# Starting the split normed inputs of a hybrid decoder layer 192 bytes into longer tiles

## The chip, the cores and the metric

The kernel runs on one core of one Trainium2 chip. The metric is the device time of one execution in microseconds (us). Five engines work side by side, each through its own list of instructions in order: TensorE (PE: matmuls; its weight loads are listed as PEld), VectorE (DVE), ScalarE (ACT), GpSimd (POOL) and SyncE (SP, which here only issues DMAs). SBUF, the on-chip memory, has 128 partitions, and a tile takes the same range of bytes in each of them.

## The reference, cut to what matters

One decoder layer over 512 positions of width 1024, in float32. Two token mixers work on the same normed input, their results are gated and summed, and a convolutional feed-forward follows:

```python
h = rmsnorm(x, norm_mix_g[l])
proj = h @ w_in[l]
bg, cg, xv, q, k, v, z, a, b, ga, gb = jnp.split(proj, pts, axis=-1)
y_a = short_conv_branch(bg, cg, xv, conv_a_w[l]) @ w_a_out[l]
y_b = gdn_branch(q, k, v, z, a, b, ...) @ w_b_out[l]
mix = jax.nn.sigmoid(ga) * y_a + jax.nn.sigmoid(gb) * y_b
x = x + mix @ w_o[l]
h = rmsnorm(x, norm_ffn_g[l])
x = x + conv_ffn(h, w_up[l], ffn_conv_w[l], w_down[l])
```

`w_in` has 9232 columns, `w_up` 5632, and `w_down` is 2816 by 1024. `gdn_branch` is a chunked gated delta rule over 8 heads, whose decays are differences of a running sum G of log decays.

## The kernel before, in words

Every float32 operand of the large products is split in two: a rounded part (type fp32r) and the rest. A product of two split operands is three matmuls: high by low, low by high, high by high (`mm3`; all of them are recorded under line 109, in `mm`). Weights come from HBM into two buffers (`raw0`, `raw1`), or into others for the last stage. ACT rounds each 128x512 piece into `wh` (line 150) and DVE subtracts for `wl` (line 151); 12 buffers of each kind stand between them and PE.

A matmul streams its moving operand, one column after another, past a stationary operand of 128 columns. In the trace the name ahead of the comma is the moving operand and the name behind it the stationary one: `ps<-hT,wh` streams the normed input past weights, `ps<-wh,xs` streams weights past an activation.

The inputs that this text is about:

- `hT` (two tiles, `hT0` high and `hT1` low): the normed input of the mixers, turned so that a partition is a channel; 8 channel tiles of 512 positions, 16,384 bytes in a partition. It is made once in the first 30 us and read until 470 us by all products with `w_in`.
- `h2` (shown as `h` in the trace, since numbers are left out of names): the same for the feed-forward, made around 600 us and read until about 825 us by all products with `w_up`.
- `ts` and `us`: split sums and differences of quarters of `hT` and of `h2`. The jobs made by `sum_job` compute a block of the product in seven forms of half the positions (256 columns) in place of eight: three forms stream quarters of `hT` or `h2`, four stream `ts` or `us`. The jobs made by `col_job` stream all 512 columns of `hT` or `h2`.

Each job covers 256 columns of weights. `run_jobs` walks the list of jobs in a fixed order: the products with `hT` in 512 columns with the delta rule's chains between them, then jobs in sums, then the outputs of the two mixers (moving operands `yas` and `yb`), the output matrix (`mix`, `mixb` stationary), then `w_up` (512 and 256 columns mixed), then `w_down` (`xs` stationary, weights moving). Work of the other engines is put between the matmuls by a counter of streamed columns (`tick` in `mm`), so the order on each engine is fixed when the program is built.

Where a tile starts: in the built program the tiles `hT0`, `hT1`, both `h2`, `wh`, `wl`, `yas`, `yb` and `kqs` all start 224 bytes past a multiple of 256 bytes, and a channel tile or half of one begins a multiple of 1,024 bytes further on. The data of `ts` and `us` start 192 bytes into their tiles (`UP = 48` elements in `page` and `place`), and so 160 bytes past a multiple of 256.

Other users of the same memory: the tags `h0`, `h1` are taken again by the split `yb`, and the tags of `h2` by `raws`, four buffers that weights of `w_down` are loaded into. `GT` is a 32x128 tile: DVE copies the turned G into it, and a DMA writes it to DRAM (`gtd`), from which the decays of a pair of heads (`Dm`) are read back. `junk` is a 128x128 tile that ACT's squares are written to and nobody reads; the first use of it in the program is the first `front`.

Of the kernel before, what the change touches and what calls it, by code (L numbers as in the profile page):

```python
# [9 lines left out]
F32 = mybir.dt.float32  # L10
F32R = mybir.dt.float32r
# [5 lines left out]
P = 128  # L17
S = 512
NT = S // P
D = 1024  # L20
ND = D // P
# [40 lines left out]
def layer_kernel(ctx, tc, x, norm_mix_g, w_in, w_ab, conv_a_w, gdn_conv_w, gdn_A_log, gdn_dt_bias,  # L62
# [14 lines left out]
    def nm(s):  # L77
        cnt[0] += 1
        return f"{s}{cnt[0]}"

    def bank():
        return ps.tile([P, 512], F32, tag="ps", name=nm("ps"))
# [21 lines left out]
    def drain(queue):  # L104
        while queue:
            advance(queue, 1)
# [19 lines left out]
    raws = [wp.tile([P, 4, S], F32, bufs=1, name=f"raw{e}") for e in range(2)]  # L126
# [6 lines left out]
    class Block:  # L133
# [21 lines left out]
        def split(self):  # L155
            if self.ready:
                return
            self.ready = True
            for q in range(4):
                self.part(q, self.raw[:, q])  # L160
                yield
# [191 lines left out]
    UP = 48  # L353

    def place(pool_, tag, name, up=0):
        t = pool_.tile([P, ND * S + 64], F32R, tag=tag, name=name)[:, up:up + ND * S]
        return t.rearrange("p (m a n) -> p m a n", m=4, a=4)

    def split(dst, idx, src):
        act.copy(out=dst[0][:, idx], in_=src)  # L360
        dve.tensor_tensor(out=dst[1][:, idx], in0=src, in1=dst[0][:, idx].bitcast(F32), op=ALU.subtract)
# [26 lines left out]

    p1 = ExitStack()
    hp = p1.enter_context(tc.tile_pool(name="hp", bufs=1))  # L390
    hT = [hp.tile([P, ND, S], F32R, tag=f"h{i}", name=f"hT{i}") for i in range(2)]
    yb = hp.tile([P, ND, S], F32, name="yb")


# [59 lines left out]
    def next_cv():  # L454
        ncv[0] += 1
        return cvs[ncv[0] % 2]
# [201 lines left out]
    gd = p2.enter_context(tc.tile_pool(name="gd", bufs=1))  # L658

    def hn(ap):  # L660
        return ap.rearrange("p (h n) -> p h n", n=NT)

    def prep(pr):
        Dm = by_columns(page("Dm", "Dm"), P)
        nc.sync.dma_start(out=Dm, in_=gtd[8 * pr:8 * pr + 8, :].partition_broadcast(P))
        pool.affine_select(out=Dm, in_=Dm, compare_op=ALU.is_ge, fill=-1e30, base=0,
                           pattern=[[0, 8], [1, P]], channel_multiplier=-1)
        Dms[pr] = Dm
# [10 lines left out]
    def gates_chain(o):  # L679
        abT = next_cv()[0:32]  # L680
        act.copy(out=abT, in_=o[0:32, :])
        yield
        o2 = bank()
        for n in range(NT):
            pe.transpose(out=o2[:, n * 32:(n + 1) * 32], in_=abT[:, n * P:(n + 1) * P], identity=ident[:32, :32])
        ab4 = o2[:, 0:128].rearrange("p (n c) -> p c n", c=32)
        abv = gd.tile([P, 16, NT], F32, name="abv")
        dve.tensor_copy(out=abv, in_=ab4[:, 16:32])
        dve.tensor_tensor(out=abv, in0=abv, in1=ab4[:, 0:16], op=ALU.add)
        T = lambda n: gd.tile([P, 32], F32, tag=n, name=nm(n))  # L690
        u, t, z, q, g = T("u"), T("t"), T("z"), T("q"), T("g")
        dve.tensor_tensor(out=hn(u), in0=abv[:, 0:8, :], in1=dtb.unsqueeze(2).broadcast_to([P, H, NT]), op=ALU.add)
        tc.keep_in_program_order(act.activation(out=hn(beta), in_=abv[:, 8:16, :], func=AF.Exp, scale=-1.0))
        tc.keep_in_program_order(act.activation(out=alg, in_=alg, func=AF.Exp))
        dve.tensor_scalar(t, u, -1.0, None, op0=ALU.mult)
        dve.tensor_tensor(out=t, in0=t, in1=u, op=ALU.min)
        tc.keep_in_program_order(act.activation(out=t, in_=t, func=AF.Exp))
        yield
        pool.tensor_scalar(beta, beta, 1.0, None, op0=ALU.add)
        pool.tensor_scalar(z, t, 2.0, None, op0=ALU.add)  # L700
        yield
        dve.reciprocal(out=beta, in_=beta)
        dve.reciprocal(out=z, in_=z)
        dve.tensor_scalar(u, u, 0.0, None, op0=ALU.max)
        yield
        pool.tensor_tensor(out=t, in0=t, in1=z, op=ALU.mult)
        pool.tensor_tensor(out=z, in0=t, in1=t, op=ALU.mult)
        pool.tensor_scalar(q, z, 1.0 / 15.0, 1.0 / 13.0, op0=ALU.mult, op1=ALU.add)
        for c in (11, 9, 7, 5, 3, 1):
            pool.tensor_tensor(out=q, in0=q, in1=z, op=ALU.mult)  # L710
            pool.tensor_scalar(q, q, 1.0 / c, None, op0=ALU.add)
        pool.tensor_tensor(out=q, in0=q, in1=t, op=ALU.mult)
        pool.tensor_scalar(q, q, 2.0, None, op0=ALU.mult)
        pool.tensor_tensor(out=g, in0=q, in1=u, op=ALU.add)
        pool.tensor_tensor(out=hn(g), in0=hn(g), in1=alg.unsqueeze(2).broadcast_to([P, H, NT]), op=ALU.mult)
        pool.tensor_scalar(g, g, -1.0, None, op0=ALU.mult)
        for _ in range(Y_G):
            yield
        o3 = bank()
        pe.matmul(o3[:, 0:32], lhsT=triu, rhs=g, start=True, stop=True)  # L720
        pe.matmul(o3[:, 32:64], lhsT=ones, rhs=g, start=True, stop=True)
        G, Gl = T("G"), T("Gl")
        dve.tensor_copy(out=G, in_=o3[:, 0:32])
        dve.tensor_copy(out=Gl, in_=o3[:, 32:64])
        dve.tensor_scalar(negG, G, -1.0, None, op0=ALU.mult)
        dve.tensor_tensor(out=kdv, in0=Gl, in1=G, op=ALU.subtract)
        act.activation(out=kdv, in_=kdv, func=AF.Exp)
        act.activation(out=eGl, in_=Gl, func=AF.Exp)
        act.activation(out=eG, in_=G, func=AF.Exp)
        dve.tensor_scalar(neG, eG, -1.0, None, op0=ALU.mult)  # L730
        yield
        o4 = bank()
        pe.transpose(out=o4[0:32, 0:P], in_=G, identity=ident)
        GT = gd.tile([32, P], F32, name="GT")
        dve.tensor_copy(out=GT, in_=o4[0:32, 0:P])
        nc.sync.dma_start(out=gtd, in_=GT)
        prep(0)

    def use_ab():
        ab_products(o_ab, HS, S)  # L740
        chains.append(Task(gates_chain(o_ab)))
# [9 lines left out]
    def tl(n, b=1, shape=(P, 8, P)):  # L751
        return gd.tile(list(shape), F32, tag=n, bufs=b, name=nm(n))
# [396 lines left out]
    st = {}  # L1149
# [118 lines left out]
    def split_ya():  # L1268
        st["yas"] = [Rows([by_columns(page(n, "yas", F32R)) for n in names])
                     for names in (("kq0", "KU0"), ("AV0", "vT", "Dm"))]  # L1270
        for k in range(ND):
            split(st["yas"], k, st["ya"][:, k, :])
            yield

    def split_yb():
        st["yb"] = [hp.tile([P, ND, S], F32R, tag=f"h{i}", name=f"yb{i}") for i in range(2)]
        for k in range(ND):
            split(st["yb"], k, yb[:, k, :])
            yield
# [5 lines left out]
    def start_split_yb():  # L1285
        drain(splits)
        drain(evacs)
        evacs.append(Task(split_yb()))
# [123 lines left out]
    def open_o():  # L1412
        drain(evacs)
        p1.close()
        fp = ctx.enter_context(tc.tile_pool(name="fp", bufs=1))
        st["x1"] = fp.tile([P, NT, D], F32, name="x1")
        st["fp"] = fp
        st["h2"] = [fp.tile([P, ND, S], F32R, tag=f"h2{i}", name=f"h2{i}") for i in range(2)]
        s7 = st["s7"] = p7.enter_context(tc.tile_pool(name="s7", bufs=2))
        gff = st["gff"] = s7.tile([P, D], F32, name="gff", bufs=1)  # L1420
        nc.sync.dma_start(out=gff, in_=norm_ffn_g[0].partition_broadcast(P))
        for t in range(NT):
            nc.sync.dma_start(out=st["x1"][:, t, :], in_=x2[t * P:(t + 1) * P, :])
# [42 lines left out]
    def o_first(p):  # L1466
        def use(wh, wl):
            if p == 0:
                open_o()
                open_banks(o_banks, ("v2", "v3", "v1", "11"))  # L1470
                st["mixb"] = [slots(page("CT", "mixb", F32R)), Rows([slots(page(n, "mixb", F32R)) for n in ("vT", "Dm")])]
            if p == 2:
                splits.append(Task(prep_b(mix_pairs(0), *mix_b(0))))
                splits.append(Task(prep_b(mix_pairs(2), *mix_b(2))))
            times_a(o_banks, st["mix", p // 2], p % 2, wh, wl, p == 0, p == ND // 2 - 1)
        return use
# [19 lines left out]
    def raw():  # L1496
        return raw_block()
# [229 lines left out]
    def down_place(i):  # L1727
        def p():
            if i < 2:
                return raw()  # L1730
            if "raws" not in st:
                st["raws"] = [st["fp"].tile([P, 2, 4, S], F32, tag=f"h2{e}", name=f"raws{e}") for e in range(2)]
            e = (i - 2) % 4
            return st["raws"][e // 2][:, e % 2]
        return p
# [61 lines left out]
```

## Time and profile before

| | |
|---|---|
| median of 3 runs | 949.34 us (948.34 to 950.11) |
| the profiled execution: time, span | 949.49 us, 947.8 us |
| mean granted TensorE clock | 0.996 |
| PE busy | 934.4 us, 99% |
| DVE busy | 778.8 us, 82% |
| ACT busy | 546.9 us, 58% |
| POOL busy | 166.4 us, 18% |
| bytes moved by DMA | 138.23 MB, mean 146 GB/s |

The span runs from the first to the last instruction; the execution's own time is 1.7 us longer. PE's busy time is the union of its matmuls with modelled ends, and consecutive matmuls overlap in it, so the duration of a matmul in a row (some 280 ns with 256 columns, 390 with 512) is longer than what it costs. What a matmul costs PE is the distance between the start of one and the start of the next, and that is read from the timeline, where each row begins with a start.

### The profile page before, as it was taken

How to read it: one execution, taken by the hardware profiler on the slowest of the kernel's cores; microseconds unless marked ns; L12 is line 12 of the kernel's file. 1: busy time of each engine (PE TensorE's matmuls, PEld its weight loads, DVE VectorE, ACT ScalarE, POOL GpSimd, SP SyncE). 2: the span in 40 equal slices, each digit the busy share in tenths (PEclk: the TensorE clock that was granted, in tenths of full speed). 3: DMA queues.
4: the chain of work that ended last, by engine and by line, in shares of the span. 5: the costliest groups of instructions: out<-in, count | busy, mean ns of one | idle time of the engine just before them, and what ended most of it. 6: DMA issues, size and time to landing. Idle time of an engine off the chain costs nothing. (4 is left out here: it accounts for less than half of the span.)

```text
span 947.8 us, 17650 instructions
## 1 busy us (share of the span) xinstructions
PE 934.4 (99%) x6512; PEld 826.8 (87%) x6512; DVE 778.8 (82%) x1448; ACT 546.9 (58%) x1202; POOL 166.4 (18%) x280
## 2 busy tenths in 40 slices
PE   8999999999999999999999999999999999999996
PEld 6888887887889999999988888988899998888885
DVE  5978686898978998899753579999899899968875
ACT  6796756666465654555741246466565556556563
POOL 3330401304110022222322000321313110000000
PEclk9999999999999999999999999999999999999999
DMA  6443412213021477776987345575776865087322
GB/s 231 157 139 100 122 54 90 76 50 102 9 91 46 127 191 164 185 197 174 290 219 171 97 153 205 164 191 178 179 174 193 177 135 178 1 294 240 109 91 89
DMA packets 78679, 138.23 MB, mean 146 GB/s; under 512 B 24667, under 2 KB 25600, under 8 KB 76032
## 3 DMA queue, kind: packets, MB, share of 16 engines
q1 hardware_dynamic: 65904, 107.47, 34.8%
q0 software_dynamic: 12544, 29.37, 16.1%
q8 instruction: 51, 0.84, 0.3%
q14 instruction: 36, 0.29, 0.1%
q10 hardware_dynamic: 144, 0.26, 0.1%
HBM read 133.64 MB, written 32.78 MB: 176 GB/s over the span
## 5 line engine op out<-in xcount | busy, mean ns | idle before, releaser
L150 ACT CAST wh<-raw 128x512 fp32r<-128x512 f32 x377 | 223.2, 620 | 184.0 <-PE ps L109 115.3
L109 PE MATMUL ps<-hT,wh 128*128 128x512 f32 (+1 forms) x1048 | 283.1, 350 | 1.1 <-ACT hT L570 0.8
L151 DVE TENSOR_TENSOR wl<-raw,wh 128x512 fp32r<-128x512 f32 x377 | 250.6, 685 | 36.3 <-ACT wh L150 33.1
L109 PEld LDWEIGHTS ps<-hT,wh 128*128 128x128 f32 x1048 | 183.4, 190 | 21.6 <-ACT hT L570 1.1
L109 PE MATMUL ps<-hT,wl 128*128 128x512 f32 (+1 forms) x524 | 172.5, 343 | 0.0
L109 PE MATMUL ps<-h,wh 128*128 128x256 f32 (+1 forms) x688 | 168.4, 333 | 0.0
L109 PEld LDWEIGHTS ps<-h,wh 128*128 128x128 f32 x688 | 118.5, 189 | 12.5
L109 PEld LDWEIGHTS ps<-hT,wl 128*128 128x128 f32 x524 | 99.6, 190 | 9.7
L109 PE MATMUL ps<-h,wl 128*128 128x256 f32 (+1 forms) x344 | 108.0, 332 | 0.0
L109 PE MATMUL ps<-ts,wh 128*128 128x256 f32 x544 | 100.8, 280 | 0.0
L109 PE MATMUL ps<-wh,xs 128*128 128x512 f32 (+1 forms) x320 | 96.6, 384 | 0.0
L109 PEld LDWEIGHTS ps<-ts,wh 128*128 128x128 f32 x544 | 85.1, 188 | 0.4 <-ACT u L338 0.2
L173 DVE TENSOR_TENSOR raw<-raw 128x512 f32<-128x512 f32 x108 | 74.2, 687 | 2.0
L109 PEld LDWEIGHTS ps<-h,wl 128*128 128x128 f32 x344 | 65.2, 189 | 6.2
L109 PEld LDWEIGHTS ps<-wh,xs 128*128 128x128 f32 x320 | 59.7, 188 | 11.8
L109 PE MATMUL ps<-ts,wl 128*128 128x256 f32 x272 | 65.7, 277 | 0.0
L109 PE MATMUL ps<-wl,xs 128*128 128x512 f32 (+1 forms) x160 | 61.5, 384 | 0.0
L237 POOL COPY gate<-raw 1x1 f32<-1x1 f32 x38 | 15.6, 411 | 254.2 <-DMA raw<-in_w_up_dram 100.1
L109 PE MATMUL ps<-us,wh 128*128 128x256 f32 x320 | 58.2, 278 | 0.7 <-ACT v L341 0.7
L367 DVE SCALAR_TENSOR_TENSOR ct<-ps,wA,ct 128x511 f32<-128x511 f32 (+2 forms) x72 | 53.1, 740 | 4.0 <-ACT ct L364 3.8
L150 ACT CAST wh<-raws 128x512 fp32r<-128x512 f32 x66 | 39.6, 620 | 25.6 <-DVE wl L151 8.1
L151 DVE TENSOR_TENSOR wl<-raws,wh 128x512 fp32r<-128x512 f32 x66 | 43.2, 686 | 11.6 <-ACT wh L150 11.5
(340 smaller groups left out, 1641.0 us busy)
## 6 DMA issues: line engine op xcount, KB each, us to landing
raw<-in_w_up_dram SPq DMA_DIRECT2D x88, 256.0 KB, 4.4
raw<-in_w_in_dram SPq DMA_DIRECT2D x20, 1024.0 KB, 5.1
raw<-in_w_in_dram SPq DMA_DIRECT2D x64, 256.0 KB, 4.5
dv<-in_w_down_dram POOLq DMA_DIRECT2D x50, 256.0 KB, 6.5
raws<-in_w_down_dram SPq DMA_DIRECT2D x32, 256.0 KB, 3.7
raws<-dv SPq DMA_DIRECT2D x24, 256.0 KB, 5.3
ov<-in_w_o_dram POOLq DMA_DIRECT2D x20, 256.0 KB, 6.2
raw<-in_w_a_out_dram SPq DMA_DIRECT2D x16, 256.0 KB, 5.0
```

The lines of the kernel that those rows point to most:

```text
L109: pe.matmul(o, lhsT=a, rhs=b, start=start, stop=stop, skip_group_check=free)
L150: act.copy(out=wh, in_=src)
L151: dve.tensor_tensor(out=wl, in0=src, in1=wh.bitcast(F32), op=ALU.subtract)
L173: dve.tensor_tensor(out=r[q], in0=a, in1=b, op=op)
L237: tc.keep_in_program_order(pool.tensor_copy(out=gate[:, 0:1], in_=el[:, 0:1]))
L367: dve.scalar_tensor_tensor(out=dst[:, sh:], in0=src[:, :S - sh], scalar=wcol(j), in1=dst[:, sh:], op0=ALU.mult, op1=ALU.add)
```

## The change

`rows_at` makes a tile of 16,640 bytes in a partition and returns 16,384 bytes of it, `up` elements from its start. `hT` and `h2` are made by it with `up=UP`, 48 elements or 192 bytes; the split `yb` and `raws`, which share their tags, are made by it with `up=0`, so that all users of a tag have one size. The 512 bytes that the two longer mixer tiles take are had by dropping `GT`: the turned G is copied into the first 32 partitions of a `junk` tile.

```diff
+    def rows_at(pool_, tag, name, up=0, dtype=F32R):
+        t = pool_.tile([P, ND * S + 64], dtype, tag=tag, name=name)[:, up:up + ND * S]
+        return t.rearrange("p (k n) -> p k n", n=S)
...
-    hT = [hp.tile([P, ND, S], F32R, tag=f"h{i}", name=f"hT{i}") for i in range(2)]
+    hT = [rows_at(hp, f"h{i}", f"hT{i}", UP) for i in range(2)]
...
-        GT = gd.tile([32, P], F32, name="GT")
+        GT = tl("junk", 1, (P, P))[0:32]
         dve.tensor_copy(out=GT, in_=o4[0:32, 0:P])
         nc.sync.dma_start(out=gtd, in_=GT)
...
-        st["yb"] = [hp.tile([P, ND, S], F32R, tag=f"h{i}", name=f"yb{i}") for i in range(2)]
+        st["yb"] = [rows_at(hp, f"h{i}", f"yb{i}") for i in range(2)]
...
-        st["h2"] = [fp.tile([P, ND, S], F32R, tag=f"h2{i}", name=f"h2{i}") for i in range(2)]
+        st["h2"] = [rows_at(fp, f"h2{i}", f"h2{i}", UP) for i in range(2)]
...
-                st["raws"] = [st["fp"].tile([P, 2, 4, S], F32, tag=f"h2{e}", name=f"raws{e}") for e in range(2)]
+                st["raws"] = [rows_at(st["fp"], f"h2{e}", f"raws{e}", dtype=F32).rearrange("p (a q) n -> p a q n", a=2)
+                              for e in range(2)]
```

In the built program the data of `hT0`, `hT1` and of both `h2` then start 160 bytes past a multiple of 256 bytes, as those of `ts` and `us` do; `yb`, `raws`, `wh` and `wl` start 224 past one as before. What lies behind the longer tiles moves up by 256 or 512 bytes. On every engine the same instructions stand in the same order as before. One wait is added: the first ACT square that writes `junk` also waits for the DMA that reads the turned G out of it.

## The prediction

> **What bounds the kernel now.** I read the page first.
>
> ```profile
> span 947.8 us, 17650 instructions
> PE 934.4 (99%) x6512; PEld 826.8 (87%) x6512; DVE 778.8 (82%) x1448; ACT 546.9 (58%) x1202; POOL 166.4 (18%) x280
> PEclk9999999999999999999999999999999999999999
> ```
>
> PE is busy 99% of the span at full clock in every slice, so a matmul that costs PE less shortens the run, as long as the others keep up. How many matmuls stream a tile that is moved is in the groups with the shapes kept apart:
>
> ```profile
> L109 PE MATMUL ps<-hT,wh 128*128 128x512 f32 x576 | 189.3, 401 | 0.0
> L109 PE MATMUL ps<-h,wh 128*128 128x512 f32 x320 | 99.8, 390 | 0.0
> L109 PE MATMUL ps<-hT,wh 128*128 128x256 f32 x472 | 94.3, 287 | 1.1 <-ACT hT L570 0.8 <-DVE hT L574 0.3
> L109 PE MATMUL ps<-h,wh 128*128 128x256 f32 x368 | 69.8, 284 | 0.0
> L109 PE MATMUL ps<-hT,wl 128*128 128x512 f32 x288 | 112.8, 392 | 0.0
> L109 PE MATMUL ps<-hT,wl 128*128 128x256 f32 x236 | 59.7, 283 | 0.0
> L109 PE MATMUL ps<-h,wl 128*128 128x512 f32 x160 | 62.3, 390 | 0.0
> L109 PE MATMUL ps<-h,wl 128*128 128x256 f32 x184 | 45.7, 282 | 0.0
> ```
>
> With 512 columns: 576 + 288 = 864 on `hT` and 320 + 160 = 480 on `h2` (here `h`), 1,344 in all. With 256 columns: 472 + 236 = 708 on `hT` and 368 + 184 = 552 on `h2`. Of the 708, those in the sums are 612 (408 + 204), by the same view between 270 and 470 us:
>
> ```profile
> L109 PE MATMUL ps<-hT,wh 128*128 128x256 f32 x408 | 79.4, 284 | 0.0
> L109 PE MATMUL ps<-hT,wl 128*128 128x256 f32 x204 | 50.7, 281 | 0.0
> ```
>
> The other 96 stand in the first block of K.
>
> **What a start is worth, in this trace.** The durations above are modelled and overlap, so I take distances between starts from PE's timeline. In one job of sums, the same kind of matmul streams first `hT`, which starts 224 bytes past a multiple of 256, and then `ts`, which starts 160 past one; and in the feed-forward first `us` (160), then `h2` (224). These are the first rows of stretches of 24 matmuls, and of what follows each:
>
> ```profile
> 374.28 0.28 PE L109 MATMUL ps<-hT,wh 128*128 128x256 f32 x1
> ...
> 377.14 0.29 PE L109 MATMUL ps<-ts,wh 128*128 128x256 f32 x1
> ...
> 379.88 0.28 PE L109 MATMUL ps<-hT,wh 128*128 128x256 f32 x1
> ```
>
> ```profile
> 705.29 0.28 PE L109 MATMUL ps<-us,wh 128*128 128x256 f32 x1
> ...
> 708.03 0.28 PE L109 MATMUL ps<-h,wh 128*128 128x256 f32 x1
> ...
> 710.89 0.28 PE L109 MATMUL ps<-us,wh 128*128 128x256 f32 x1
> ```
>
> 24 on `hT` take 2.86 us, 119.2 ns each, and 24 on `ts` 2.74 us, 114.2 ns. 24 on `us` take 2.74 us and 24 on `h2` 2.86 us. So it is 5.0 ns a matmul, in two places, with shape, type and kind of stationary operand the same. That it goes with the start and not with the smaller pages of `ts` is shown by a third kind, weights as the moving operand, which also start at 224:
>
> ```profile
> 936.49 0.28 PE L109 MATMUL ps<-wl,xs 128*128 128x256 f32 x1
> 936.61 0.40 PE L109 MATMUL ps<-wh,xs 128*128 128x256 f32 x2
> 936.85 0.28 PE L109 MATMUL ps<-wl,xs 128*128 128x256 f32 x1
> ```
>
> These take 0.12 us each (one from 936.49, two from 936.61 to 936.85), like `hT` and `h2`. With 512 columns on `h2`, 15 matmuls take 3.40 us between the next two rows, 226.7 ns each:
>
> ```profile
> 641.95 0.39 PE L109 MATMUL ps<-h,wl 128*128 128x512 f32 x1
> ...
> 645.35 2.09 PE L109 MATMUL ps<-h,wh 128*128 128x512 f32 x9
> ```
>
> **The change, part by part.**
>
> *256 columns.* `hT` and `h2` come to start where `ts` and `us` do, so I take the whole distance: (612 + 552) x 5.0 = 5.8 us. The 96 early ones run while inputs are still arriving, and I count half of them: 0.2 us. Together 6.0.
>
> *512 columns.* No row streams 512 columns from a start of 160, so this is the unknown cost. At 224 the two lengths give 226.7 and 119.2 ns: 256 columns more cost 107.5 ns, and so 119.2 - 107.5 = 11.7 ns of either do not grow with the length. At 160 the same working leaves 114.2 - 107.5 = 6.7 of them. A part that does not grow with the length should shrink by the same 5.0 ns at 512 columns as at 256; the end of a stretch of 512 columns also lies at the same place in its 256 bytes as that of 256. The bounds of a gain: 0 (the 512-column rate is set by something else), and 11.7 ns (all that does not grow vanishes). Nothing excludes a loss either, since no row has this start and length; its size would be at most a second such part, 11.7 ns more. I take a gain of 5.0, since the nearest rows are those with the same operands at 256 columns: 1,344 x 5.0 = 6.7 us, with a gain and a loss of 15.7 as ends.
>
> The page "TensorE: Matmul & The Clock Gate" of the Trainium skill gives, under "Back-to-back issue gap", N / 2.4 + 2.5 ns from one matmul to the next, with nothing for where an operand starts: 109.2 ns at N = 256 and 215.8 at 512. The trace shows 119.2 or 114.2 and 226.7, so the rule misses both the size and the difference; by it the sum would be zero.
>
> *What takes some of it back.* PE runs ahead only if weights are split in time and chains end in time. The stretches are: delta rule until 270 us, sums until 470, the first block of `w_up` until 640, the rest until 830.
>
> ```profile
> 100.00:200.00 100.00, 99.48 (x931) 83.58 (x931) 77.20 (x216) 63.54 (x203) 24.32 (x36) 1.00 0.24 70
> 270.00:470.00 200.00, 200.00 (x1773) 195.06 (x1772) 175.71 (x301) 118.95 (x267) 42.07 (x73) 1.00 0.61 164
> 600.00:640.00 40.00, 40.00 (x277) 37.38 (x276) 39.35 (x58) 22.01 (x38) 12.60 (x18) 1.00 0.70 180
> 640.00:830.00 190.00, 189.28 (x1244) 173.38 (x1243) 177.35 (x273) 110.80 (x206) 30.50 (x50) 1.00 0.59 152
> ```
>
> The columns behind the length are busy times of PE, PEld, DVE, ACT and POOL. In the sums DVE has 24 us to spare and PE would save 3 to 4. From 640 to 830 DVE has 12.6 us to spare and PE would save about 4.2: (552 - 192) x 5.0 + 480 x 5.0, less the few that lie outside; 192 are in the first block (by the code, two jobs of two banks, two halves and 24 matmuls). Who waits there for whom:
>
> ```profile
> ACT wh L150 <- PE ps L109: 28.3, 18, 3.4
> ```
>
> ACT stands 28.3 us waiting until PE gives buffers of weights back, so the split is held up by PE and speeds up with it. At one place it is the other way round, and the chain that ended last runs through it:
>
> ```profile
> 765.84 5.49 DMA raw<-in_w_up_dram
> ...
> 776.35 0.38 ACT v L341
> ```
>
> A load starts there when DVE has given back its buffer, ACT waits for it, and PE for a copy behind it on ACT. In the 20 us before, two jobs of sums follow each other, and PE will reach that wait earlier by what it gains in them: 2 jobs x 3 forms x 12 matmuls x 5.0 ns = 0.36 us, lost. From 600 to 640 us DVE is busy 39.35 of 40 us; the 192 matmuls there are worth 1.0 us, and I count half as lost, 0.5. In the delta rule PE's busy time is already short of the window by 0.5 us in 100; its chains do not get shorter, and I take 0.5 us off. Together -1.4.
>
> *The turned G in `junk`.* The copy and the DMA stay as they are. The added wait holds ACT's first square, and behind it all of ACT's list, until the DMA has read the tile:
>
> ```profile
> L736 SPq DMA_DIRECT2D gtd<-GT x1: 324/324/324, 46.3 to 46.3; - x1
> DMA to landing us min/median/max: 1.4/1.4/1.4
> L777 ACT ACTIVATE junk<-ps x32: 266/278/315, 50.1 to 215.5; 128x128 f32<-128x128 f32 x32
> ```
>
> Issued at 46.3 and landed 1.4 us later, 47.7; the square starts at 50.1. The wait is over 2.4 us before it is asked for: 0. Without that cover, ACT would stand for as long as the landing is late.
>
> *Split `yb`, `raws` and what is moved up.* The first two start where they did, modulo 256, and so does everything behind the longer tiles: 0. The writers of `hT` and `h2` (ACT, DVE) write the same bytes elsewhere; `ts` is written at the new start already, with nobody waiting for it: 0.
>
> Sum: -6.0 - 6.7 + 1.4 = -11.3 us. Against the profiled execution, 949.49 us (span 947.8 and 1.7 around it), that is 938.2; the median of the runs shown is 0.15 lower, so I say 938.0 us.
>
> **Rivals.**
>
> *512 columns gain nothing.* For it: no row with 512 columns at any other start shows that 226.7 ns can be undercut. Against it: the same part that shrinks at 256 columns, 11.7 ns, is in the 226.7 as well. Then only the 256 columns gain: 949.3 - 6.0 + 0.9 (the losses of the second and fourth stretch) = 944.2 us.
>
> *All 512-column overhead goes, and nothing is lost:* 949.3 - 6.0 - 15.7 = 927.6 us. Nothing in the trace shows a matmul without it; I give it little.
>
> *The start does nothing.* Then `ts` and `us` are cheaper for another reason, such as their own neighbourhood, and the change moves tiles alone: 949.3 us. Against it: three kinds of operand at 224 and two at 160 fall on two values. The Trainium skill's page "SBUF — State Buffer" says under "Operand start alignment" that its rule is about legality, not speed, and that its runs timed nothing; it leaves this open, and the matmul page's gap speaks for it.
>
> *Slower: 512 columns cost more from the new start.* If a stretch of 2,048 bytes from 160 costs a second such part, 11.7 ns more than from 224, the 864 + 480 lose 15.7 us and the 256 columns gain 6.0: 949.3 + 15.7 - 6.0 + 0.9 = 959.9 us (losses as in the first rival). It turns slower where 512 columns take up the 5.1 us that are left of the gain: 5.1 / 1,344 is 3.8 ns, or 230.5 ns a matmul. For it speaks only that the rows with the new start all have 256 columns.
>
> *DVE becomes the bound of the feed-forward.* If its idle time from 600 to 830 can't be used at all, the 552 and about 470 there give nothing: what is left is 612 x 5.0 + 0.2 + 864 x 5.0 - 0.5 = 7.1, so 942.2 us. Against it: those 28.3 us of ACT waiting for PE.
>
> **Chances.** My forecast, with a gain at both lengths (934 to 941.5): 0.70. Gain at 256 columns alone: 0.14. DVE as the bound: 0.05. Overhead all gone: 0.02. No effect: 0.05. Slower: 0.04. The range leaves out the last three and reaches from 933 (both lengths at 6 ns and no losses: 2,508 x 6 = 15.0, or 934.3, and some way to the case below) to 944.6. About 0.2% is what a measurement of this kernel can tell from no change. Faster by more: 0.70 + 0.14 + 0.05 + 0.02 = 0.91; within: 0.05; slower: 0.04.
>
> **What would show it.** In the timeline after, 24 matmuls on `hT` or `h2` with 256 columns should take 2.74 us in place of 2.86, and 15 on `h2` with 512 columns 3.32 or 3.33 in place of 3.40; those on `yb`, `ts`, `us` and on weights should not change. The count of PE's waits should grow by little, at ACT's copies (line 341) and in the delta rule. The prediction is wrong if 512 columns still take 226.7 ns, or if PE's waits take back more than 1.4 us, to be seen as waits on `wl` or on ACT's copies.

## The result: 953.71 us, slower by half a per cent

The changed kernel takes 953.71 us (median of 5 runs, 952.71 to 954.22) against 948.74 us (948.34 to 950.11) for the kernel before, timed beside it: a ratio of 1.0048 with a 95% interval of 1.0034 to 1.0063. The prediction was 938.0 us, faster; the change is slower by 5.0 us, outside the range. In the profiled execution after (953.71 us too) the span grew by 4.2 us:

```profile
span 952.0 us, 17651 instructions
PE 936.7 (98%) x6512; PEld 820.1 (86%) x6512; DVE 779.3 (82%) x1448; ACT 547.0 (57%) x1202; POOL 171.0 (18%) x280
```

PE is still the bound. The two groups below, with the shapes kept apart, answer to the same groups in the prediction. With 512 columns the mean of one went from 401 to 406 ns, with 256 from 287 to 280: one length lost, the other gained.

```profile
L109 PE MATMUL ps<-hT,wh 128*128 128x512 f32 x576 | 191.9, 406 | 0.0
...
L109 PE MATMUL ps<-hT,wh 128*128 128x256 f32 x472 | 90.2, 280 | 0.3 <-DVE hT L578 0.3
```

PE's timeline after shows the cost from start to start. 256 columns, in the sums:

```profile
374.10 0.28 PE L109 MATMUL ps<-ts,wh 128*128 128x256 f32 x1
...
376.82 0.28 PE L109 MATMUL ps<-hT,wh 128*128 128x256 f32 x1
...
379.54 0.28 PE L109 MATMUL ps<-ts,wh 128*128 128x256 f32 x1
```

24 matmuls on `hT` take 2.72 us, 113.3 ns each, where they took 2.86; 24 on `ts` take the same 2.72. That is the gain which the prediction counted on. 512 columns, the stretch on `h2` that the prediction showed (15 matmuls from the first row to the second):

```profile
645.23 0.39 PE L109 MATMUL ps<-h,wl 128*128 128x512 f32 x1
...
648.73 2.15 PE L109 MATMUL ps<-h,wh 128*128 128x512 f32 x9
```

3.50 us in place of 3.40: 233.3 ns a matmul, 6.6 more than before, where a gain of 5.0 was predicted. The whole trace is summed up by lining up the same matmuls of both executions and comparing the time from each start to the next; where one such time differs by more than 60 ns it is counted as a wait. From 29 us on, the 512 columns cost 7.0 us more (4.0 on `hT`, 3.1 on `h2`), the 256 columns 5.3 less (2.6 and 2.7), and waits add 3.5. At 29 us the changed kernel was 0.9 us ahead, as was e2 below, which moves no start. Together these come to 4.3, against the 4.2 measured; the waits are taken up below.

### The profile page after: what moved, and what is told of

Same layout as the page of the kernel before. It is cut to its first block, busy times and chain, and to the rows that moved or that the text cites. A ratio compares the mean times of both kernels' runs of the same rounds, so it can differ in the third digit from the quotient of the medians.

```text
span 952.0 us, 17651 instructions
## 1 busy us (share of the span) xinstructions
PE 936.7 (98%) x6512; PEld 820.1 (86%) x6512; DVE 779.3 (82%) x1448; ACT 547.0 (57%) x1202; POOL 171.0 (18%) x280
## 5 line engine op out<-in xcount | busy, mean ns | idle before, releaser
L150 ACT CAST wh<-raw 128x512 fp32r<-128x512 f32 x377 | 223.2, 620 | 191.9 <-PE ps L109 113.6
L109 PEld LDWEIGHTS ps<-hT,wh 128*128 128x128 f32 x1048 | 181.2, 188 | 23.1 <-DVE hT L578 0.5
L237 POOL COPY gate<-raw 1x1 f32<-1x1 f32 x38 | 21.1, 556 | 250.3 <-DMA raw<-in_w_up_dram 95.6
```

The costliest lines, as they stand in the source:

```text
L109: pe.matmul(o, lhsT=a, rhs=b, start=start, stop=stop, skip_group_check=free)
L150: act.copy(out=wh, in_=src)
L237: tc.keep_in_program_order(pool.tensor_copy(out=gate[:, 0:1], in_=el[:, 0:1]))
```

## The experiments

The question was first what sets the 233.3 ns, then why the gain at 256 columns is not all seen in the time. The code below is shortened; `...` and lines that are all comment stand for what is not shown.

**Does the cost go with the moving operand's start? (e1_starts)** The layer is left out; only matmuls of the layer's kind run, in groups of 24, one for each pair of starts:

```diff
+    # eight moving tiles: 0, 32, ... 224 bytes past a multiple of 256 (movea to moveh)
+    # three stationary ones: 224, 160 and 0 past one (kepta, keptb, keptc)
+    for kept in "abc":
+        for cols in (512, 256):
+            for move in "abcdefgh":
+                group(move, kept, cols)     # 24 matmuls
```

> It leaves the whole layer out and streams matmuls alone: groups of 24 at each of eight starts (0, 32, ... 224 past a multiple of 256 bytes; tiles movea to moveh), with 512 and with 256 columns, each with stationary operands that start at 224, 160 and 0 (tiles kepta, keptb, keptc). Theory A (the start alone sets a matmul's cost, differently for the two lengths): with stationary operands at 224, 512 columns take 226.7 ns from 224 and 231 to 236 from 160, and 256 columns 119 to 120 from 224 and 114 from 160, as in the layer. Rival B (the cost comes from other engines' or DMAs' traffic, which meets the operands at other places after the change): 160 and 224 take the same here, within 1 ns, at each length. If the start of the stationary operand matters too, the three sets of groups differ; if not, they agree within 1 ns. Other starts: open; a start with less than 226.7 at 512 and less than 119 at 256 would make a better kernel.

Measured, in PE's timeline; a group's time is the distance to the next row:

```profile
45.47 5.75 PE L72 MATMUL psy<-movef,kepta 128*128 128x512 f32 x24
51.06 5.75 PE L72 MATMUL psy<-moveg,kepta 128*128 128x512 f32 x24
56.65 5.61 PE L72 MATMUL psy<-moveh,kepta 128*128 128x512 f32 x24
62.09 2.96 PE L72 MATMUL psz<-movea,kepta 128*128 128x256 f32 x24
...
76.16 2.89 PE L72 MATMUL psz<-movef,kepta 128*128 128x256 f32 x24
78.89 3.00 PE L72 MATMUL psz<-moveg,kepta 128*128 128x256 f32 x24
81.72 3.04 PE L72 MATMUL psz<-moveh,kepta 128*128 128x256 f32 x24
84.59 5.77 PE L72 MATMUL psy<-movea,keptb 128*128 128x512 f32 x24
...
112.62 5.63 PE L72 MATMUL psy<-movef,keptb 128*128 128x512 f32 x24
118.09 5.77 PE L72 MATMUL psy<-moveg,keptb 128*128 128x512 f32 x24
...
143.30 3.04 PE L72 MATMUL psz<-movef,keptb 128*128 128x256 f32 x24
146.17 3.00 PE L72 MATMUL psz<-moveg,keptb 128*128 128x256 f32 x24
```

`movef` starts at 160. Beside `kepta` (224), as in the changed kernel, it takes 5.59 us for 24 of 512 columns, 232.9 ns, and 2.73 us for 24 of 256, 113.8 ns. Beside `keptb`, whose start is also 160, the same tile takes 5.47 us (227.9 ns) and 2.87 us (119.6 ns). `moveh` (224) beside `kepta` (224), as in the kernel before, takes 5.44 us (226.7) and 2.87 (119.6). So it is not the moving start that counts but its distance from the stationary one; from here on, distance is moving start less stationary start, modulo 256 bytes. Distance 0 is best for 512 columns and among the worst for 256; distance 192, which the change makes, is the other way round. The rival that other engines' traffic does it is refuted: from 17 us on no other engine worked here, and the rates are those of the layer within 1 ns.

**How far does each distance go? (e5_distances)** The same without the layer, 32 matmuls a group, one stationary start and 26 moving ones, down to steps of 4 bytes:

```diff
+    # distances 0, 4, 8, 12, 16, 24, 32, 48, 56, 60, 64, ... 192, 196, 200, 208, 256, 320, 448, 504, 508 bytes
+    for cols in (512, 256):
+        for d in distances:
+            group(moving[d], kept, cols)        # 32 matmuls
```

> It leaves the whole layer out. 32 matmuls in a row at each of 26 distances, modulo 512 bytes, from the start of the stationary operand to that of the moving one (0 to 508, some of them no multiple of 32; tile mov64at starts 64 behind), with 512 and with 256 columns; one place of the stationary tile for all. Theory C (the distance between the two operands' starts sets the cost), from the first microbenchmark: with 512 columns 227 ns at 0 and 256, 229.4 at 64 and 320, 233 to 234 at 32, 96, 128, 160, 192, 448; with 256 columns 119.9 at 0 and 256, 113.3 at 64, 113.7 at 192 and 448, 118 at 32 and 320, 118.7 at 128, 117.4 at 160. Rival A (the moving start alone): the costs of 0, 64, 192 here are those that the starts 128, 192 and 64 had there with the first stationary tile, 234, 233 and 234 with 512 columns. Distances that are no multiple of 32: open; if the unit is 32 bytes or more, 4 to 28 behave as 0 or 32.

```profile
143.97 7.62 PE L65 MATMUL psy<-mov192at,kept 128*128 128x512 f32 x32
151.43 7.81 PE L65 MATMUL psy<-mov196at,kept 128*128 128x512 f32 x32
159.08 7.58 PE L65 MATMUL psy<-mov200at,kept 128*128 128x512 f32 x32
...
174.00 7.43 PE L65 MATMUL psy<-mov256at,kept 128*128 128x512 f32 x32
181.27 7.50 PE L65 MATMUL psy<-mov320at,kept 128*128 128x512 f32 x32
```

With 512 columns, 32 matmuls take 7.46 us at 192 bytes (233 ns), 7.65 at 196 (239), 7.27 at 256 (227). Four bytes move it by 6 ns. Over all distances 512 columns lay between 227.1 ns (at 256) and 239.0 (at 68 and 196); the group at 0, which ran first and took 287 ns, is not counted. 256 columns lay between 113.3 (at 16) and 122.8 (at 4). None was best for both lengths. At 64 bytes 256 columns took 117.8, not the 113.3 that was expected.

**Do the longer tiles, `junk` and the moved neighbours cost anything? (e2_long_tiles) And which part of the change costs what? (e3_h2_only, e4_hT_only)** All three are the changed kernel with starts put back:

```diff
-    hT = [rows_at(hp, f"h{i}", f"hT{i}", UP) for i in range(2)]
+    hT = [rows_at(hp, f"h{i}", f"hT{i}") for i in range(2)]         # e2, e3
...
-        st["h2"] = [rows_at(fp, f"h2{i}", f"h2{i}", UP) for i in range(2)]
+        st["h2"] = [rows_at(fp, f"h2{i}", f"h2{i}") for i in range(2)]  # e2, e4
```

> The change with the start left at 0: tiles 256 bytes longer, everything behind moved up, the turned G in junk, but hT and h2 start 224 past a multiple of 256 as before. Theory A (the starts are the whole effect): as before, 948.7 us, within 0.7. Rival B (the moved tiles, or the wait of ACT's first square on the DMA out of junk): 952 to 954 as after the change.

> Only h2 starts 192 bytes later. Theory A: before 602 us nothing changes, behind it the change cost 1.2 us (distance between the two traces 3.0 us at 602 and 4.2 at 842): 949.9 us. Rival B: 953 to 954.

> Only hT starts 192 bytes later. Theory A: the 3.0 us that the change had lost by 602 us: 951.7 us, with three waits of PE on ACT (line 338) of some 0.6 us each between 440 and 460 us. Rival B: 953 to 954.

Against 948.78 us for the kernel before on the same chip:

| | median, us | ratio, 95% interval |
|---|---|---|
| e2, longer tiles alone | 949.07 | 1.0000 (0.9988 to 1.0012) |
| e3, `h2` moved | 950.39 | 1.0018 (1.0003 to 1.0033) |
| e4, `hT` moved | 952.14 | 1.0030 (1.0017 to 1.0042) |

The longer tiles, the turned G in `junk` and what moves up cost nothing that can be measured. The two starts add up: 1.61 + 3.36 = 4.97 us, and the change measured 953.71 - 948.74 = 4.97. Each of these is known to about 1.3 us either way, so that they agree to the last digit is luck. Where the time goes is seen by lining up the same matmuls of two executions and noting how far the later one falls behind in each stretch (us; stretches in the time of the kernel before):

| | 29 to 275 | 275 to 440 | 440 to 477 | 628 to 771 | 771 to 781 | 781 to 824 |
|---|---|---|---|---|---|---|
| the change | +3.17 | -1.43 | +2.15 | -0.29 | +0.66 | +0.71 |
| e2, longer tiles | +0.01 | -0.11 | +0.43 | 0.00 | +0.71 | 0.00 |
| e3, `h2` moved | +0.02 | -0.11 | -0.02 | -0.29 | 0.00 | +0.71 |
| e4, `hT` moved | +3.17 | -1.42 | +2.72 | 0.00 | +0.74 | +0.01 |

From 29 to 275 nearly all columns on `hT` come 512 at a time: all loss. From 275 to 440 the sums gain 1.4. From 440 to 477 more than that is lost again. The 0.7 at 771 to 781 stands in e2 as well, where no start moves, so it does not need the moved starts. Two stretches are not in the table: from 477 to 628 the change gains 0.1 and e3 0.5, and behind 824 both lose 0.3. The part of `h2` is not settled by this table: behind 29 us, e3's trace is only 0.05 us slower in all, since the 256 columns on `h2` gain what the 512 columns lose (3.1 us each). Its execution took 947.90 us, 2.5 below e3's median, so what the median loses is not in this trace. By 29 us it was 1.7 us ahead of the kernel before, long before `h2` is made; the granted clock in that stretch was 1.00, as in the change and in e2, and 0.94 in the profiled execution of the kernel before.

**Is it the distance in the layer too? (e6_weights_moved)** The kernel before, with no activation moved; the buffers of the split weights alone are pushed up by 64 bytes, and `GT` gives the room:

```diff
     nraw = [0]
+    wp.tile([P, 16], F32, bufs=1, name="padlow")
...
+    wp.tile([P, 48], F32, bufs=1, name="padhigh")
...
-        GT = gd.tile([32, P], F32, name="GT")
+        GT = tl("junk", 1, (P, P))[0:32]
```

> The kernel before, with no activation moved: a pad of 64 bytes ahead of the buffers of wh and wl and one of 192 behind them, and the turned G in junk to make room. All matmuls of hT and h2 then have the distance 192 modulo 256 that the change gave them, ts and us have 128, yas and yb 192, and weights streamed past xs and mix 64. Theory C: with 512 columns hT and h2 lose 6.5 ns x 1,344 = 8.7 us and yas and yb 6.5 x 384 = 2.5, xs and mix 2.6 x 624 = 1.6; with 256 columns ts and us lose 4.7 x 1,296 = 6.1, and hT and h2 gain 5.5 x 1,164 = 6.4: 948.7 + 12.5 = 961 us, 957 to 964. Rival A (the start of the moving operand alone): all these start where they did, except the streamed weights; 626 of these with 512 columns, at 5 ns: 952 us at most.

960.34 us against 948.80, ratio 1.0121 (1.0102 to 1.0139), where the distance asked for 961 and the moving start for 952 at most. The distance is confirmed in the layer. That the sum came so close is in part luck: lined up as above, 512 columns on `hT` and `h2` lost 6.9 us in place of 8.7, and 256 columns on them gained 3.5 in place of 6.4, and the two errors partly cancel. 24 matmuls of 512 columns on `h2` (first two rows) take 5.60 us, 233.3 ns, with `h2` where it always was; `ts`, whose start did not move either, takes 2.85 us for 24 (118.8 ns) where it took 2.74:

```profile
641.75 2.26 PE L109 MATMUL ps<-h,wh 128*128 128x512 f32 x9
...
647.35 2.26 PE L109 MATMUL ps<-h,wh 128*128 128x512 f32 x9
```

```profile
374.42 0.28 PE L109 MATMUL ps<-ts,wh 128*128 128x256 f32 x1
...
377.27 0.28 PE L109 MATMUL ps<-hT,wh 128*128 128x256 f32 x1
...
380.10 0.28 PE L109 MATMUL ps<-ts,wh 128*128 128x256 f32 x1
```

**Two tries to have both rates (e7_distance_64, e8_sum_weights_moved, and e9_ring_alone).** e7 puts `hT` and `h2` at a distance of 64 bytes:

```diff
-        t = pool_.tile([P, ND * S + 64], dtype, tag=tag, name=name)[:, up:up + ND * S]
+        up, more = (16 if up else 0, 16) if tag[-1] == "0" else (0 if up else 112, 112)
+        t = pool_.tile([P, ND * S + more], dtype, tag=tag, name=name)[:, up:up + ND * S]
```

> The change with both parts of hT and of h2 starting 64 bytes behind the weights modulo 512, in place of 192 and 448. Theory C: with 512 columns 229.4 ns in place of 226.7 before, 2.7 x 1,344 = +3.6 us; with 256 columns 113.4 in place of 119.2, 5.8 x 1,164 = -6.8 us; the waits of the change at the end of the sums, up to 2.0 us, stay: 947.5 us, 945.5 to 949. Rival A: the start is 32 modulo 256 for the moving operand, where nothing was known before the first microbenchmark; by its first set of groups 229.5 and 113.3, the same time. This run is for the better version, not to tell A from C.

950.77 us against 948.80, ratio 1.0019 (1.0004 to 1.0033). In unbroken stretches from 353 us on, 512 columns took 228.9 to 229.3 ns as expected, and in the jobs of sums 256 columns took 117.7 to 118.1 and not 113.4: a miss, with the rate that e5 shows at 64.

e8 leaves `hT` and `h2` at distance 0 and moves only the weights of the jobs in sums up by 64 bytes, in two rings that replace the weight buffers; `ts` and `us` go to their tiles' start. e9 is the control: the rings with nothing moved.

```diff
+    rings = [wp.tile([P, WQ * S + 64], F32R, bufs=1, name=n) for n in ("wh", "wl")]
...
-            wh = wp.tile([P, S], F32R, tag="wh", bufs=WQ, name=nm("wh"))
-            wl = wp.tile([P, S], F32R, tag="wl", bufs=WQ, name=nm("wl"))
+            wh, wl = slot(0, self.late), slot(1, self.late)   # 64 bytes up where late
...
     class SumBlock(Block):
+        late = True       # e8; False in e9
```

> hT and h2 stay where they were; ts and us start where their tiles start; the buffers of wh and of wl are one ring each, and the weights of jobs in sums are written 64 bytes further on in it (one of the 12 places is left out where other weights follow them). Then the distance is 0 or 256 for all 512-column matmuls, as before, and 192 or 448 for the 256-column matmuls of the sums on hT and h2 (612 + 360) and for ts and us. The turned G is in junk. Theory C (the distance sets the cost): the 972 gain 5.5 ns each, 5.3 us; at most 2.0 us go to waits at the end of the sums as after the change: 945.4 us, 943.0 to 947.5. Rival A (the moving start alone): ts and us, now at 224, lose 5.0 ns x 1,296 = 6.5 us and nothing gains: 955 us.

> The same rings, but no weights are moved and ts and us start 192 bytes into their tiles as before: the control for the ring of the run beside it. Both theories: as before, 948.8 us within 1.0; if it is off by more, the ring's own part is taken out of the other result.

e9 took 949.61 us against 949.25, ratio 1.0001 (0.9987 to 1.0015): rings cost nothing. e8 took 962.64, ratio 1.0142 (1.0114 to 1.0169), a second miss. 512 columns were back at 226 to 227 ns, but at distance 192 the 256 columns of `hT`, `h2`, `ts` and `us` all took about 117.7. Lined up with the kernel before, these rates make 3.0 of the 16.2 us that its trace loses behind 29 us. The rest is nearly all waits and slow matmuls behind them. PE's longest waits in e8 (in total, how many, the longest), and the window behind the longest (its length, then busy PE, PEld, DVE, ACT, POOL, then the granted clock):

```profile
PE ps L109 <- ACT v L354: 5.7, 3, 3.2
```

```profile
789.10:795.00 5.90, 5.88 (x26) 5.82 (x27) 2.75 (x5) 1.48 (x4) 0.52 (x1) 0.52 0.56 47
```

Behind a wait of 3.2 us the granted clock was 0.52, and 24 matmuls of 256 columns took 220 ns each. Ahead of that wait ACT stood 5.90 us for a load of `w_up`. It may be that loads come late because a place of a ring overlaps two of the other kind where moved and unmoved weights follow each other, and comes free later; no run shows it.

So one distance, 192, gave 113.3 in one kernel and 117.7 in another.

**One distance, two rates (e10_two_parts, e11_entries).** e10, without the layer, tried whether it hangs on how the high and the low part lie to each other; groups of 48 matmuls with the layer's order of high and low, starts modulo 512:

```diff
+CASES = ((480, 480, 160, 160), (480, 480, 160, 416), (480, 224, 160, 416), ...   # stationary high, low; moving high, low
+         ..., (480, 480, 480, 480), (480, 480, 160, 160), ...)                   # the first once more, as the tenth
```

> It leaves the whole layer out. Groups of 48 matmuls in the layer's pattern (high by low and low by high in turn, four pairs, then four of high by high), the two parts in tiles of their own, whose starts modulo 512 are set: first twelve groups with 256 columns, then eight of the same with 512. It asks why the last run but one took 117.7 ns for 256 columns at distances 192 and 448, where the layer and the first two microbenchmarks took 113.3 to 114.8. Theory C1 (the distances of moving and stationary operand alone, 192 or 448 are fast): all groups but the ninth (distance 0: 119 to 120) and the last two (64) take 113.3 to 114.8 with 256 columns. Rival C2 (it also matters whether the two stationary parts start at the same place modulo 512, or 256 apart as in that run): the groups with 480, 224 and 32, 288 take 117 to 118, those with 480, 480 and 32, 32 take 113.3 to 114.8. Rival C3 (the absolute start matters too): the four groups with stationary starts of 32 take 117 to 118, and those with 480 take 113.3 to 114.8. With 512 columns all of these distances take 231 to 236 by each theory.

None of the three theories holds: the first eight groups of 256 columns all took 117.8 ns, 512 columns 233.2 in all eight. The slow rate held through those eight groups, 384 matmuls in 45 us. But the tenth group, with the first one's starts, took 5.46 us for 48 (113.8 ns) where the first took 5.65 (117.7). Ahead of the first stood 512 columns at distance 0, ahead of the tenth 256 columns at distance 0. e11 repeats one group at distance 192 behind different entries:

```diff
+        for turn in range(2):
+            for case, cols in ((even, 512), (even, 256), (off, 512), (far, 256), (far, 512)):   # distances 0, 0, 192, 64, 64
+                group("y", case, cols, 2)      # 24 matmuls: the entry
+                group("z", off, 256, 4)        # 48 matmuls at distance 192: the group
```

> The layer is left out. Groups of 48 matmuls of 256 columns at distance 192 (moving start less stationary start), all of the same two tiles, each behind another entry of 24 matmuls: 512 columns at distance 0, 256 at 0, 512 at 192, 256 at 64, 512 at 64; the whole row of five twice; at the end behind 12 of 512 at distance 0 and behind 12 of 256 at 0. In the run before, such a group took 117.8 ns a matmul behind 512 columns at distance 0, and 113.3 behind 256 at 0. Theory H, what ran just before decides, and the rate is then kept: 117.8 behind 512 at 0 and 113.3 behind 256 at 0, in both turns, and at the end again, since 12 matmuls are entry enough; of the other three entries it says only that both turns agree (12 groups: at least 5.4 us for 48 or 5.7, nothing between). Rival T, the place in time (the first groups of a program, or the clock, or tiles written a short while ago): the first groups 117.8, the later ones 113.3 whatever stands ahead of them, so the turns differ. Rival N, it can't be foreseen: neither order.

PE's timeline, second turn and end; `move160` rows are the groups, the others the entries, again from row to row:

```profile
66.95 0.39 PE L77 MATMUL psy<-move480l,kept480h 128*128 128x512 f32 x1
...
72.39 0.28 PE L77 MATMUL psz<-move160l,kept480h 128*128 128x256 f32 x1
...
78.05 0.28 PE L77 MATMUL psy<-move480l,kept480h 128*128 128x256 f32 x1
...
80.92 0.29 PE L77 MATMUL psz<-move160l,kept480h 128*128 128x256 f32 x1
...
86.38 0.39 PE L77 MATMUL psy<-move160l,kept480h 128*128 128x512 f32 x1
...
91.97 0.28 PE L77 MATMUL psz<-move160l,kept480h 128*128 128x256 f32 x1
...
97.42 0.28 PE L77 MATMUL psy<-move32l,kept480h 128*128 128x256 f32 x1
...
119.57 0.28 PE L77 MATMUL psz<-move160l,kept480h 128*128 128x256 f32 x1
...
125.22 0.28 PE L77 MATMUL psx<-move480l,kept480h 128*128 128x256 f32 x1
```

Behind 512 columns at distance 0 the group takes 5.66 us, 117.9 ns each (5.65 in the first turn, and 5.65 from 119.57 behind an entry of only 12); behind 256 at distance 0, 5.46 (5.45 in the first, and 113.7 ns again in the last group, behind an entry of 12); behind 512 at distance 192, 5.45 (5.44). The other two: behind 256 at 64, 5.44 and 5.45; behind 512 at 64, 5.65 both times. Both turns agree in all five, so what ran before sets the rate, and the group keeps it for its 48 matmuls. The place in time does not. Why an entry does so was not tried. The last 24 matmuls are not always the whole of it: in e7, `us` (distance 192) follows 24 matmuls of 256 columns and, ahead of them, 48 or more of 512, all at distance 64, at 650.61 and again at 671.51; it took 117.8 ns a matmul the first time and 113.6 the second.

This fits e8 from 364 us on: there the sums follow 48 matmuls of 512 columns at distance 0, and everything in them streams at distance 192 and keeps the slow rate. Its first sums, from 303 us, are slow too, but stand behind the short matmuls of the chains, an entry that no run tried. The two rates are also seen inside the changed kernel.

## Why the prediction was wrong, point by point

**The step that failed: "a part that does not grow with the length should shrink by the same 5.0 ns at 512 columns as at 256".** It gave -6.7 us. Measured: +7.0. The rate is not a length plus a constant part of the start. It hangs on the distance of the two operands, and between distances 0 and 192 the two lengths go opposite ways (e1: 226.7 to 232.9 with 512 columns, 119.6 to 113.8 with 256). The prediction had the loss as its slower rival at a chance of 0.04, with 11.7 ns a matmul and the turn at 230.5; it was 6.6 ns and 233.3 in the stretch shown, and 5.2 ns over all 1,344. All rows with 512 columns had distance 0 before, so the profile could not show it; but the absence of such a row deserved far more than 0.04.

**The cause behind it was taken too narrowly.** "That it goes with the start and not with the smaller pages" was right as far as it went. What the rows of before could not part is the moving start from its distance: all stationary operands started at 224. Weights as moving operand, the prediction's third kind, stood at distance 0 too. e1 and e6 part them.

The Trainium skill's page "TensorE: Matmul & The Clock Gate" gives under "Back-to-back issue gap", for a single isolated matmul, its length plus 2.5 ns, with no term for a start: 215.8 and 109.2 ns. No group of e1 or e5 came down to that; the fastest were 226.7 and 113.3. The Trainium skill's page "SBUF — State Buffer" says under "Who interferes with whom" that PE waits on nobody. e1 fits this as far as other engines go, since with none of them at work its rates were those of the layer, but PE's rate is not independent of where its own two operands begin: in e6, moving the weights alone cost 1.21%. That the weight load's reads meet the moving ones is a guess that no run here tests.

**256 columns: -6.0 predicted, -5.3 measured, and by another road.** Of the 6.0, 5.8 lay behind 29 us, where the 5.3 are counted. In the fast stretches they came down further than forecast, to 113.3 in place of 114.2, and `ts` and `us` with them. In others the whole job ran at the slow rate. After a short wait of PE in the changed kernel's sums:

```profile
320.65 0.39 PE L109 MATMUL ps<-ts,wh 128*128 128x256 f32 x1 [0.21 <-ACT u L338]
...
322.17 0.28 PE L109 MATMUL ps<-hT,wh 128*128 128x256 f32 x1
...
336.30 0.28 PE L109 MATMUL ps<-hT,wh 128*128 128x256 f32 x1
...
339.13 0.28 PE L109 MATMUL ps<-ts,wh 128*128 128x256 f32 x1
...
356.09 0.39 PE L109 MATMUL ps<-hT,wh 128*128 128x512 f32 x1
```

24 on `hT` take 2.83 us, 117.9 ns, and so does all from 322.17 to 356.09, 33.92 us. The same matmuls took 33.46 us before, with `ts` at 114.2 and `hT` at 119.2:

```profile
320.16 0.28 PE L109 MATMUL ps<-hT,wh 128*128 128x256 f32 x1
...
353.62 0.39 PE L109 MATMUL ps<-hT,wh 128*128 128x512 f32 x1
```

Here the change gains nothing, and loses 0.46. Then 512 columns run at distance 192, and behind them the sums take 113.3, which is the order that e11 shows. That the wait started the slow stretch is seen, not tested. Of PE's other three waits in the sums, one is followed by a slow stretch (459.54) and one by a fast one (442.77); behind the third (449.06) 36 matmuls are slow, but the same 36 were slow before too, without a wait.

**The sums' gain was handed back, more than was counted.** The prediction took off 1.4 us in all; the waits behind 29 us came to 3.5, of which 1.1 are in e2 as well, where no start moves. It took off 0.36 us at 757 to 776, where nothing is seen but the 0.7 that e2 has too, and nothing at the end of the sums, where PE had no wait before:

```profile
437.00:462.00 25.00, 25.00 (x214) 24.76 (x213) 21.11 (x34) 18.00 (x39) 7.73 (x16) 1.00 0.78 234
```

The same window after (busy PE, PEld, DVE, ACT, POOL behind the length), and in the timeline there PE's three waits:

```profile
437.00:462.00 25.00, 23.45 (x199) 22.76 (x198) 22.65 (x37) 15.53 (x34) 7.36 (x15) 1.00 0.75 233
```

```profile
442.77 0.38 PE L109 MATMUL ps<-ts,wh 128*128 128x256 f32 x1 [0.52 <-ACT u L343]
...
449.06 0.38 PE L109 MATMUL ps<-ts,wh 128*128 128x256 f32 x1 [0.56 <-ACT u L338]
...
459.54 0.39 PE L109 MATMUL ps<-ts,wh 128*128 128x256 f32 x1 [0.47 <-ACT u L338]
```

PE loses 1.55 us in these 25. It waits for copies on ACT. Ahead of the first two, ACT stood behind DVE; ahead of the third, it stood 2.02 us for a load of weights (last row of ACT's timeline):

```profile
441.83 0.62 ACT L150 CAST wh<-raw 128x512 fp32r<-128x512 f32 x1 [3.19 <-DVE raw L173]
442.36 0.37 ACT L343 COPY u<-ps 128x256 f32<-128x256 f32 x1
...
458.08 0.62 ACT L150 CAST wh<-raw 128x512 fp32r<-128x512 f32 x1 [2.02 <-DMA raw<-in_w_a_out_dram]
```

```profile
438.45 1.29 DVE L1246 TENSOR_TENSOR ya<-o,c 128x512 f32<-128x512 f32 x2
439.65 0.69 DVE L151 TENSOR_TENSOR wl<-raw,wh 128x512 fp32r<-128x512 f32 x1
440.38 2.15 DVE L173 TENSOR_TENSOR raw<-raw 128x512 f32<-128x512 f32 x3
```

DVE works there without a gap: from 427 to 457 us it was busy 28.87 of 30 us before and 29.21 after. So by the trace DVE is the bound ahead of the first two waits, and PE that comes earlier only waits; no run gave DVE less to do. The prediction read 24 us of DVE's idle time in a window of 200 us; that mean hid a nearly full stretch of some 30. How much a run loses there varies: +0.43 us in e2, where no start moves, +2.72 in e4.

**What held.** The longer tiles, the turned G in `junk`, split `yb` and `raws`: 0 predicted, 0 in e2 within 1.1 us. Nearly so the first block of `w_up`, where half of 1.0 us was counted as lost: from 602 to 628 us the change gains 0.14, since a wait of PE takes back 0.4, the slow starts around it included; e3 gains 0.5 there. `yb`, `yas`, `xs` and `mix` with 512 columns kept their 226 to 227 ns.

## What to carry to other kernels

Where a matmul brings its own stationary operand each time, look at where the two operands start to each other, for each length of the moving operand by itself: a rate read at one length says nothing of another. Before moving a tile, ask which rows have the new combination at all; an effect that one small kernel of matmuls can measure in 200 us should not be carried over from one shape to another by a sum. And slack is read in windows as short as the buffers are deep: an engine with 12% idle over 200 us can be full where the gain has to pass.

## What the runs showed of the hardware that was not expected

- A matmul of this kind (fp32r, each with its own load of 128 columns of weights) cost 226.7 to 239.0 ns with 512 columns and 113.3 to 122.8 with 256 in e1 and e5, where nothing but the starts was changed from group to group; 4 bytes moved it by 6 ns (192 to 196). With 256 columns, part of this can be what ran before.
- The distance counts modulo 256 bytes: in e5, 64 and 320 took 229.2 and 229.4 with 512 columns, and 117.8 and 117.9 with 256; 192 and 448 took 233.2 and 233.4, and 113.9 and 113.5.
- At distance 192, 256 columns have two rates, 113.3 and 117.8 ns, and what ran before chooses. Distance 64 took 113.3 once in e1 and 117.7 to 118.1 elsewhere in groups and jobs of sums. In all three sets of e1 it stood behind 24 matmuls of 256 columns at distance 32; ahead of those came 512 columns at distance 0 in the set that took 113.3, and 256 columns at distance 0 in the others. Whether that made the difference stays open.
- Behind a wait of PE of 3.2 us in e8 the granted clock was 0.52 over 5.9 us, and matmuls took 220 ns in place of 118; behind the changed kernel's waits, of up to 0.8 us, it was 1.00.
- No kernel here beat the one before. One that has 512 columns at distance 0 and enters the sums through 256 columns at distance 0 before it goes to 192 was not tried.
